# Second attention of a two-branch encoder layer: exponentials copied by ScalarE's DMA queue into a tile of the rounded type, transposed from there later in the tile; 15-row ranges

## The chip, the cores and the metric

The kernel runs on one core of one Trainium2 chip. The metric is the device time of one launch in microseconds. A core has five engines with a queue of instructions each: TensorE (PE, with its weight loads shown apart as PEld), VectorE (DVE), ScalarE (ACT), GpSimd (POOL) and SyncE (SP), which here only issues DMAs. Other engines can issue DMAs as well; before the change ACT does so twice, at the start.

## The reference

One layer over two sequences of 2048 tokens (x_prompt, x_sample) with 1024 features. All is float32.

```
h    = rms_norm(x) * norm_w
q_a | k_a | v_a | g_a | q_b | k_b | v_b | g_b = h @ w_in          # 3328 columns
A: windowed attention, 8 query heads on 2 key heads, +-128 tokens, norms, rotary, a sink per head
B: 8 heads on a grid of 32 rows x 64 columns; a query sees 8 rows x 16 columns around it
   q_b, k_b = rms_norm(q_b), rms_norm(k_b)
   s  = q_b . k_b / 8 + rpb_b[row offset, column offset];  p = softmax(s);  o_b = p @ v_b
x = x + concat(o_a * silu(g_a), o_b * silu(g_b)) @ w_out
y = x + (p @ w_ple) * sigmoid(x @ w_ple_gate)
```

## The kernel before, in words

Products are made in split form: a float32 operand is kept as a part rounded to PE's faster type (F32R in the code, fp32r in the profile's casts) and a rest, and three products of these parts are added (`project`, line 257). Casts and subtractions that make the two parts run on ACT, DVE and POOL.

The work has three stages. Tiles f = 0 to 31 are the first attention (about 0 to 800 us), tiles f = 32 to 95 the second (about 800 to 1815 us), and then follows the output stage. While a tile of attention runs, PE also makes projections for later tiles (the products `pq`, `pg`, and in the second attention `pqk`, `pvg`, at the end `pple`); they are a stream from which `paired` (line 1054) lets so many columns run and then puts in the next piece of the attention, after a plan. PLAN_B is that plan: a share of the tile, whether the piece belongs to the tile itself (1) or to the one before it (0), its kind and its index. All PE instructions stand in the order that the program writes them (`pinned`, line 237). The other engines' orders are made by a scheduler, but for the instructions marked `P(...)`, which stay where the program puts them.

A tile of the second attention (`unit_b`, line 845) has 128 queries (8 rows by 16 columns of the grid), four heads, and a window of keys of `nr` rows by 24 or 32 columns. Its pieces for each head: `sc` makes the scores in PSUM (`scb`, two products) and adds the bias and takes the maximum on DVE (`softmax`, line 264, into a tile `s` of which there are five); `exp` makes the four exponentials in place on ACT (`exps`, line 275, in the head order 0, 2, 1, 3) and then loads the values (`vw`); `pt` transposes the exponentials by 3 or 4 chunks of keys into one PSUM bank (`ptb`, with the identity in another row order, `rowwise`, as the moving operand), from which ACT makes the rounded part and DVE the rest (`p_t`, lines 899 and 900); `po` multiplies with the values (`pob`); `fin` applies the gate. `po` of the last two heads runs in the tile after. `prep` readies the queries and keys of a later tile (`pqtb`, `pktb`; L837, L755 and L756), and `proj_b` takes in the projections (`vb`, `qg`; L811, L820).

Where the window has 32 columns and the block of rows is not at the edge, `nr` is 16 and the scores are 512 columns wide; with 24 columns it is 15 and they are 360 wide.

`ptb`, `scb` and `pgtb` share three PSUM banks, `pob`, `pqtb` and `pktb` two, the projections three. SP issues all loads and stores of the stages: weight blocks (`ws`), tokens (`stx`), biases, values (`vw`, `v_d`). A DMA of SP or ACT takes the next of eight landing counters (DMAHW0 to DMAHW7 in the rows below), and is issued when the DMA that had that counter before has landed. At the start the identity `ident` and `rowwise` are made in F32 by POOL, and the input stages are loaded in an order that the scheduler makes.

Of the kernel before, what the change touches and what calls it, by code (L numbers as in the profile page):

```python
# [25 lines left out]
ROW_WIN = {0: (0, 12, 12), 1: (4, 16, 15), 2: (12, 16, 15), 3: (20, 12, 12)}  # L26
# [3 lines left out]
def window(b, cb):  # L30
    c0, nc_ = COL_WIN[cb]
    r0, wide, narrow = ROW_WIN[b]
    nr = wide if nc_ == 32 else narrow
    rows = 5 if nr == 15 else 4
    return r0, nr, c0, nc_, rows

# [9 lines left out]
def query_rows(b, cb, j):  # L46

    r0, _, _, _, rows = window(b, cb)
    k0 = r0 + rows * j
    see = [r for r in range(8) if k0 - 7 <= min(max(8 * b + r - 4, 0), 24) <= k0 + rows - 1]  # L50
    return (see[0], max(see[-1] + 1, 4)) if see[0] == 0 else (min(see[0], 4), see[-1] + 1)


def bias_offsets():
# [28 lines left out]
TW = 512  # L83
# [13 lines left out]
    (0.45, 1, "pt", 0), (0.52, 1, "pt", 1), (0.60, 1, "pt", 2), (0.66, 1, "po", 0), (0.74, 1, "pt", 3), (0.80, 1, "po", 1),  # L97
# [3 lines left out]
def emit(ctx, tc, io):  # L101
# [9 lines left out]
    ident = cp.tile([128, 128], F32, tag="ident", name="ident")  # L111
    make_identity(nc, ident)

    rowwise = cp.tile([128, 128], F32, tag="rowwise", name="rowwise")
    nc.gpsimd.tensor_copy(rowwise.rearrange("p (r c) -> p r c", c=16), ident.rearrange("p (c r) -> p r c", r=8))
# [138 lines left out]
    def tr(out, in_, eye=ident):  # L254
        pinned(nc.tensor.transpose(out, in_, eye))  # L255
# [19 lines left out]
    def exps(sm, fct, gs, sink=None):  # L275

        mx, nm, den, rd, ss = (sm[k] for k in ("mx", "nm", "den", "rd", "s"))
        if sink is None:
            nc.vector.tensor_scalar_mul(nm, mx, -1.0)  # L279
            yield  # L280
        else:
            nc.vector.scalar_tensor_tensor(out=nm, in0=mx, scalar=-1.0, in1=sink[1], op0=ALU.mult, op1=ALU.min)
        for n_, i in enumerate((0, 2, 1, 3) if sink is None else range(4)):
            ex = nc.scalar.activation(ss[i], ss[i], AF.Exp, bias=nm[:, i:i + 1], accum_out=den[:, i:i + 1])  # L284
            if sink is None and n_ == 0:
                P(ex)
        if sink is not None:
# [374 lines left out]
    p_rot = []  # L662

    def unit_a(f, kv):
# [6 lines left out]
        def sc(i):  # L671
# [3 lines left out]
            if half == 0:  # L675
                pairs.append(ap.tile([128, 640], F32, tag="ev", name="s2", bufs=3))
                if not right:
                    nc.gpsimd.memset(pairs[pair][:, 256:320], 0.0)
# [166 lines left out]
    def unit_b(f):  # L845
# [5 lines left out]
        kc, nch = rows * ncol, nr // rows  # L851
# [10 lines left out]
        def load_values():  # L862
# [4 lines left out]
            for j in range(nch):  # L867
                v = four[:, j] if spare else \
                    ap.tile([128, 4, 2 * HD], F32R, tag=("vp", "vr_")[j % 2], name="vw", bufs=3 - j % 2)
                nc.sync.dma_start(v[:kc].bitcast(F32).rearrange("p h d -> p (h d)"),  # L870
                                  v_d[half, s, cb][r0 + rows * j:r0 + rows * j + rows]
                                  .rearrange("r c h a d -> (r c) (h a d)"))
                vw.append(v)
# [6 lines left out]
        def sc(h):  # L880
# [5 lines left out]
            if h == 3:  # L886
                got["ex"] = exps(sm, hr_b[:, st:st + 1], gs)
                next(got["ex"])

        def pt(x):  # L890
            h = (0, 2, 1, 3)[x]
            pt = ptile([128, 512], "pt", "ptb")
            for j in order:

                c = at[j] - 16 * sees[j][0]
                tr(pt[:kc, c:c + 128], sm["s"][h][:, kc * j:kc * j + kc], rowwise)
# [6 lines left out]
        def po(x):  # L903
# [7 lines left out]
            for j in order[::-1]:  # L911
                a, z = sees[j]
                mm(po[:, i, :].rearrange("p (a q) -> p a q", a=2)[:, :, 16 * a:16 * z], vw[j][:kc, h, :],
                   p_ts[x][:kc, :, at[j]:at[j + 1]], j == order[-1], j == order[0])
# [66 lines left out]
    made = []  # L981
# [7 lines left out]
    def ple_ahead(n, tail=False):  # L989

        load_p(n + 1)
        for m in range(KT):
# [13 lines left out]
            else:  # L1006
                ev = ap.tile([128, TW], F32, tag=("ev", "sq")[m // 2 % 2], name="ev", bufs=3 - m // 2 % 2)
# [419 lines left out]
```

## Time and profile before

| | us |
|---|---|
| runs (three) | 2465.72, 2466.20, 2466.57; median 2466.2 |
| profiled execution, its span | 2462.8 |
| PE busy | 2451.7 (100%) |
| weight loads (PEld) busy | 2075.4 (84%) |
| DVE busy | 1704.7 (69%) |
| ACT busy | 1413.1 (57%) |
| POOL busy | 856.8 (35%) |

The span runs from the first to the last instruction that the profile shows; the run's time is taken from outside and is 3.4 us more at the median. Busy times count an engine's instructions from start to end. Matmuls overlap each other in the pipeline, so that PE's 100% says that it always has a product in flight, and not how fast the products follow each other: this is told by the distance of their starts. "L255 PE ptb" is the transposition at line 255, called for the tile `ptb`. In the lines of groups, `out<-in` names the tiles; `128x368 fp32r<-128x368 f32` are output and input, partitions by elements, with their types. In the chain of waits, each row has a start, a length and the work that held the end up in that time; `x4` says that four instructions of a kind stand in the row.

### The profile page before, as it was taken

The numbers are of one execution on the slowest core, as the hardware profiler recorded it, in microseconds if no ns is written. First come the engines' busy times: TensorE is split into PE (matmuls) and PEld (weight loads), VectorE is DVE, ScalarE is ACT, GpSimd is POOL, SyncE is SP. The second block draws the span as 40 slices with busy tenths as digits, with TensorE's granted clock in tenths as the row PEclk, the third lists the DMA queues.
The fourth block names the chain that finished last, engine by engine and source line by source line (L and its number), as shares of the span: only waits on it lengthen the run. The fifth ranks groups of instructions, "written<-read, shape, count | busy, mean of one in ns | idle before, by whom it ended". The sixth has DMA issues, their size and how long they took to land.

```text
span 2462.8 us, 40532 instructions
## 1 busy us (share of the span) xinstructions
PE 2451.7 (100%) x13062; PEld 2075.4 (84%) x13062; DVE 1704.7 (69%) x4214; ACT 1413.1 (57%) x3408; POOL 856.8 (35%) x1363
## 2 busy tenths in 40 slices
PE   9999999999999999999999999999999999999999
PEld 8888888888888888888888888888888888888887
DVE  7777777777765666666666666666537655677776
ACT  6777776777664665656655566665763222344433
POOL 4555555555543544454444444443100000000000
PEclk9999999999999999999999999999999999999999
DMA  6332223332255565556955566667977445856765
GB/s 228 123 103 93 95 89 103 95 101 88 95 180 166 167 192 182 183 163 195 314 187 183 170 219 202 193 199 242 317 248 262 154 165 178 270 180 206 251 222 171
DMA packets 243316, 442.01 MB, mean 179 GB/s; under 512 B 27904, under 2 KB 82592, under 8 KB 237856
## 3 DMA queue, kind: packets, MB, share of 16 engines
q1 hardware_dynamic: 242816, 439.42, 54.8%
q8 instruction: 104, 1.70, 0.3%
q14 instruction: 108, 0.88, 0.1%
q10 hardware_dynamic: 288, 0.01, 0.0%
HBM read 309.29 MB, written 134.23 MB: 180 GB/s over the span
## 4 chain that ended last, share of the span: by engine, by line
PE 94%; DVE 2%; ACT 2%; POOL 1%; issue 1%; DMA 1%; SPq 0%; ACTq 0%; POOLq 0%; DVEq 0%
PE pvg L252 15%; PE pqk L252 14%; PE acca L1230 14%; PE accc L1230 11%; PE pg L252 6%; PE pq L252 6%; PE scb L252 4%; PE ptb L255 4%; PE pple L252 4%; PE pob L252 3%; PE po L252 3%; PE pk L252 3%; PE sc L252 3%; PE pt L255 2%; DVE pr L712 1%
## 5 line engine op out<-in xcount | busy, mean ns | idle before, releaser
L284 ACT ACTIVATE s<-s,nm 128x320 f32<-128x320 f32 (+6 forms) x512 | 294.5, 576 | 318.5 <-DVE nm L279 198.9
L252 PE MATMUL pvg<-wb,xr 128*128 128x512 f32 x1536 | 461.5, 407 | 0.0
L252 PE MATMUL pqk<-wa,xr 128*128 128x512 f32 x1536 | 442.9, 411 | 0.0
L252 PEld LDWEIGHTS pqk<-wa,xr 128*128 128x128 f32 x1536 | 266.1, 189 | 36.7
L252 PEld LDWEIGHTS pvg<-wb,xr 128*128 128x128 f32 x1536 | 266.8, 189 | 30.8
L1212 ACT CAST opd<-raw 128x512 fp32r<-128x512 f32 x224 | 131.5, 618 | 271.7 <-PE acca L1230 118.0
L353 POOL TENSOR_TENSOR xr<-stx,xr 128x512 fp32r<-128x512 f32 x186 | 238.9, 1295 | 101.3 <-ACT xr L352 76.8
L1213 DVE TENSOR_TENSOR opd<-raw,opd 128x512 fp32r<-128x512 f32 x224 | 146.7, 687 | 146.9 <-ACT opd L1212 146.9
L252 PE MATMUL pg<-wb,xr 128*128 128x512 f32 x768 | 233.3, 410 | 1.0 <-DVE vv L510 1.0
L252 PE MATMUL pq<-wa,xr 128*128 128x512 f32 x768 | 219.3, 400 | 0.0
L268 DVE CUSTOM_DVE_ANT_0 s<-scb,bias 128x288 f32<-128x288 f32 (+3 forms) x256 | 142.2, 556 | 104.6 <-PE scb L252 101.7
L137 POOL TENSOR_TENSOR yb<-vrb,power 128x8 f32<-128x8 f32 x64 | 106.4, 1662 | 222.1 <-DVE vrb L784 202.4
L1230 PE MATMUL accc<-opd,wb 128*128 128x512 f32 x768 | 176.7, 389 | 0.0
L1230 PE MATMUL acca<-opd,wa 128*128 128x512 f32 (+1 forms) x780 | 175.9, 386 | 0.5 <-ACT r L1308 0.5
L1230 PE MATMUL acca<-opd,s 128*128 128x512 f32 x768 | 175.4, 389 | 0.0
L1230 PEld LDWEIGHTS acca<-opd,wa 128*128 128x128 f32 x780 | 145.0, 188 | 30.2 <-ACT r L1308 0.7
L1230 PEld LDWEIGHTS acca<-opd,s 128*128 128x128 f32 x768 | 144.2, 188 | 29.9
L1230 PEld LDWEIGHTS accc<-opd,wb 128*128 128x128 f32 x768 | 144.2, 188 | 29.9
L919 DVE TENSOR_TENSOR otb<-pob,otb 64x512 f32<-64x512 f32 x128 | 88.1, 688 | 113.2 <-ACT otb L918 111.5
L252 PEld LDWEIGHTS pob<-p_t,vw 128*128 128x128 f32 (+2 forms) x832 | 132.6, 189 | 23.4 <-DVE p_t L900 3.4
L252 PEld LDWEIGHTS pq<-wa,xr 128*128 128x128 f32 x768 | 135.2, 189 | 17.3
L712 DVE TENSOR_TENSOR pr<-pt,pr 128x512 fp32r<-128x512 f32 (+2 forms) x248 | 135.4, 549 | 15.9 <-ACT pr L710 12.5
(171 smaller groups left out, 5169.9 us busy)
## 6 DMA issues: line engine op xcount, KB each, us to landing
stx<-x_b SPq DMA_DIRECT2D x128, 256.0 KB
vw<-v_d SPq DMA_DIRECT2D x112, 256.0 KB
stx<-x_a SPq DMA_DIRECT2D x64, 256.0 KB
stn<-x_n SPq DMA_DIRECT2D x64, 256.0 KB
v_d<-vb SPq DMA_DIRECT2D x64, 256.0 KB
ple_d<-ev SPq DMA_DIRECT2D x64, 256.0 KB
xres<-x_r SPq DMA_DIRECT2D x64, 256.0 KB
x_d<-r SPq DMA_DIRECT2D x64, 256.0 KB
```

The costliest lines, as they stand in the source:

```text
L137: nc.gpsimd.tensor_tensor(out=y, in0=v, in1=power.broadcast_to([128, n]), op=ALU.pow)
L252: pinned(nc.tensor.matmul(out, lhsT, rhs, start=start, stop=stop))
L255: pinned(nc.tensor.transpose(out, in_, eye))
L268: nc.vector.tensor_tensor_reduce(out=s, in0=ps[:, :n], in1=bias, scale=1.0, scalar=-3.0e38, op0=ALU.add, op1=ALU.max, accum_out=sm["mx"][: ...
L284: ex = nc.scalar.activation(ss[i], ss[i], AF.Exp, bias=nm[:, i:i + 1], accum_out=den[:, i:i + 1])
L353: low.tensor_tensor(out=lo, in0=raw, in1=hi.bitcast(F32), op=ALU.subtract)
L712: nc.vector.tensor_tensor(out=pr[r, 1, to], in0=pt[r, c], in1=pr[r, 0, to].bitcast(F32), op=ALU.subtract)
L919: nc.vector.tensor_tensor(out=ot[a:a + 64], in0=pq[a:a + 64], in1=ot[a:a + 64], op=ALU.add)
L1212: P(nc.scalar.copy(hi, v))
L1213: P(nc.vector.tensor_tensor(out=lo, in0=v, in1=hi.bitcast(F32), op=ALU.subtract))
L1230: pinned(nc.tensor.matmul(ps[:, cols], w[k][:, a, c:c + 128], o[:, b, cols], start=i in (0, 1, 4) and k == 0 and j == 0, stop=k == 3 and j ...
```

## The change

1. The middle blocks of rows take 15 rows of keys with 32 columns too. Their scores are 480 columns wide in place of 512, cut into chunks of 4, 4, 3 and 4 rows (`chunks`), so that the number of transpositions stays. This meets 16 of the 64 tiles.
2. `ident` and `rowwise` are of the type F32R. They are cast from an F32 identity in a pool that is closed again. A transposition of an F32 tile reads them as F32; one of an F32R tile is done in that type (`tr`).
3. For f below 90 (58 of the 64 tiles, 756 of the 832 transpositions of `ptb`), each head's exponentials are copied from `s` to one tile `tn` of type F32R, by a DMA that ACT issues. All four exponentials and the four DMAs are held in program order: exponentials 1 and 2, the first DMA, exponential 3, the second DMA, exponential 4, the last two DMAs. These are 232 DMAs of 128 rows by 288 to 480 elements. The transpositions read `tn`.
4. In PLAN_B the pieces `pt` and `po` of a tile come later: `pt` at 0.68 to 0.90 of the tile in place of 0.45 to 0.74, `po` of the first two heads at 0.86 and 0.95 in place of 0.66 and 0.80. `po` of the last two heads keeps its place in the next tile (0.09, 0.16).
5. To make room, tiles of the tag `ev` (`s2` in the first attention, `tn`, `ev` at the end) share one space as one tile of three parts.

```diff
--- before.py
+++ after.py
@@ -23,16 +23,21 @@
 NEG = -1.0e30
 EPS = 1e-6
 
-ROW_WIN = {0: (0, 12, 12), 1: (4, 16, 15), 2: (12, 16, 15), 3: (20, 12, 12)}
+ROW_WIN = {0: (0, 12), 1: (4, 15), 2: (12, 15), 3: (20, 12)}
 COL_WIN = {0: (0, 24), 1: (8, 32), 2: (24, 32), 3: (40, 24)}
 
 
 def window(b, cb):
     c0, nc_ = COL_WIN[cb]
-    r0, wide, narrow = ROW_WIN[b]
-    nr = wide if nc_ == 32 else narrow
-    rows = 5 if nr == 15 else 4
+    r0, nr = ROW_WIN[b]
+    rows = 5 if nr == 15 and nc_ == 24 else 4
     return r0, nr, c0, nc_, rows
+
+
+def chunks(nr, rows):
+
+    first = list(range(0, nr - rows, rows)) + [nr - rows]
+    return [(k, min(rows, z - k)) for k, z in zip(first, first[1:] + [nr])]
 
 
 def row_type(b):
@@ -45,9 +50,9 @@
 
 def query_rows(b, cb, j):
 
-    r0, _, _, _, rows = window(b, cb)
-    k0 = r0 + rows * j
-    see = [r for r in range(8) if k0 - 7 <= min(max(8 * b + r - 4, 0), 24) <= k0 + rows - 1]
+    r0, nr, _, _, rows = window(b, cb)
+    k, n = chunks(nr, rows)[j]
+    see = [r for r in range(8) if r0 + k - 7 <= min(max(8 * b + r - 4, 0), 24) <= r0 + k + n - 1]
     return (see[0], max(see[-1] + 1, 4)) if see[0] == 0 else (min(see[0], 4), see[-1] + 1)
 
 
@@ -94,7 +99,7 @@
 PLAN_B = (
     (0.00, 1, "sc", 0), (0.03, 1, "sc", 1), (0.07, 1, "sc", 2), (0.09, 0, "po", 2), (0.11, 1, "sc", 3), (0.16, 0, "po", 3),
     (0.16, 1, "exp", 0), (0.24, 0, "fin", 0), (0.35, 1, "prep", 0),
-    (0.45, 1, "pt", 0), (0.52, 1, "pt", 1), (0.60, 1, "pt", 2), (0.66, 1, "po", 0), (0.74, 1, "pt", 3), (0.80, 1, "po", 1),
+    (0.68, 1, "pt", 0), (0.75, 1, "pt", 1), (0.82, 1, "pt", 2), (0.86, 1, "po", 0), (0.90, 1, "pt", 3), (0.95, 1, "po", 1),
 )
 
 
@@ -108,11 +113,12 @@
         tag = PSM.get(tag, tag)
         return pp.tile(shape, F32, tag=tag, name=name, bufs=PSB[tag])
 
-    ident = cp.tile([128, 128], F32, tag="ident", name="ident")
-    make_identity(nc, ident)
-
-    rowwise = cp.tile([128, 128], F32, tag="rowwise", name="rowwise")
-    nc.gpsimd.tensor_copy(rowwise.rearrange("p (r c) -> p r c", c=16), ident.rearrange("p (c r) -> p r c", r=8))
+    ident, rowwise = (cp.tile([128, 128], F32R, tag=n, name=n) for n in ("ident", "rowwise"))
+    with tc.tile_pool(name="eye", bufs=1) as ep:
+        eye_ = ep.tile([128, 128], F32, tag="eye", name="eye")
+        make_identity(nc, eye_)
+        nc.vector.tensor_copy(ident, eye_)
+        nc.gpsimd.tensor_copy(rowwise.rearrange("p (r c) -> p r c", c=16), eye_.rearrange("p (c r) -> p r c", r=8))
     nw = cp.tile([128, KT], F32, tag="nw", name="nw")
     nc.scalar.dma_start(nw, io["norm_w"])
     ms_a = cp.tile([128, 2 * NT], F32, tag="ms_a", name="ms_a")
@@ -252,7 +258,10 @@
         pinned(nc.tensor.matmul(out, lhsT, rhs, start=start, stop=stop))
 
     def tr(out, in_, eye=ident):
-        pinned(nc.tensor.transpose(out, in_, eye))
+        if in_.dtype == F32R:
+            pinned(nc.tensor.transpose(out.bitcast(F32R), in_, eye))
+        else:
+            pinned(nc.tensor.transpose(out, in_, eye.bitcast(F32)))
 
     def project(ps, xr, w, cost):
 
@@ -272,7 +281,7 @@
     def sm_tiles():
         return {"s": [], **{k: ap.tile([128, 4], F32, tag=k, name=k, bufs=3) for k in ("mx", "nm", "den", "rd")}}
 
-    def exps(sm, fct, gs, sink=None):
+    def exps(sm, fct, gs, sink=None, turned=None):
 
         mx, nm, den, rd, ss = (sm[k] for k in ("mx", "nm", "den", "rd", "s"))
         if sink is None:
@@ -280,10 +289,18 @@
             yield
         else:
             nc.vector.scalar_tensor_tensor(out=nm, in0=mx, scalar=-1.0, in1=sink[1], op0=ALU.mult, op1=ALU.min)
+        waiting = []
         for n_, i in enumerate((0, 2, 1, 3) if sink is None else range(4)):
             ex = nc.scalar.activation(ss[i], ss[i], AF.Exp, bias=nm[:, i:i + 1], accum_out=den[:, i:i + 1])
-            if sink is None and n_ == 0:
+            if sink is None and (n_ == 0 or turned is not None):
                 P(ex)
+            if sink is None and turned is not None:
+                waiting.append(i)
+                for k in waiting[:1] if n_ in (1, 2) else waiting[:] if n_ == 3 else ():
+                    to = turned[:, k, :ss[k].shape[-1]]
+                    P(nc.scalar.dma_start(to.bitcast(F32), ss[k]))
+                    ss[k] = to
+                    waiting.remove(k)
         if sink is not None:
             es = ap.tile([128, 4], F32, tag="es", name="es", bufs=3)
             nc.vector.tensor_tensor(out=es, in0=sink[0], in1=nm, op=ALU.add)
@@ -659,7 +676,7 @@
         qrest[f] = split_q(pqt, q1, q2, 1)
         return q1, q2
 
-    p_rot = []
+    p_rot, s2, tn = [], [], []
 
     def unit_a(f, kv):
         s, t = divmod(f, NT)
@@ -673,7 +690,10 @@
             a, z = span[half]
             c0, n = 128 * t - 128 + 64 * half, z - a
             if half == 0:
-                pairs.append(ap.tile([128, 640], F32, tag="ev", name="s2", bufs=3))
+                if not s2:
+                    s2.extend([ap.tile([128, 3, 640], F32, tag="ev", name="s2", bufs=1), 0])
+                pairs.append(s2[0][:, s2[1] % 3])
+                s2[1] += 1
                 if not right:
                     nc.gpsimd.memset(pairs[pair][:, 256:320], 0.0)
             ps = ptile([128, 512], "sc", "sc")
@@ -848,7 +868,8 @@
         b, cb = divmod(j, 4)
         _, gs = held[f]
         r0, nr, c0, ncol, rows = window(b, cb)
-        kc, nch = rows * ncol, nr // rows
+        kc, ch = rows * ncol, chunks(nr, rows)
+        nch, kn = len(ch), [ncol * n for _, n in ch]
         n = nr * ncol
         if cb != 2:
             off, _ = BIAS_OFF[(row_type(b), col_type(cb))]
@@ -867,8 +888,8 @@
             for j in range(nch):
                 v = four[:, j] if spare else \
                     ap.tile([128, 4, 2 * HD], F32R, tag=("vp", "vr_")[j % 2], name="vw", bufs=3 - j % 2)
-                nc.sync.dma_start(v[:kc].bitcast(F32).rearrange("p h d -> p (h d)"),
-                                  v_d[half, s, cb][r0 + rows * j:r0 + rows * j + rows]
+                nc.sync.dma_start(v[:kn[j]].bitcast(F32).rearrange("p h d -> p (h d)"),
+                                  v_d[half, s, cb][r0 + ch[j][0]:r0 + sum(ch[j])]
                                   .rearrange("r c h a d -> (r c) (h a d)"))
                 vw.append(v)
 
@@ -884,7 +905,9 @@
                    ks_b[h % 2][:, r0:r0 + nr, h // 2, c0:c0 + ncol], j == 0, j == 1)
             softmax(h, ps, n, bias[:, h, :n], sm)
             if h == 3:
-                got["ex"] = exps(sm, hr_b[:, st:st + 1], gs)
+                if not tn:
+                    tn.append(ap.tile([128, 4, 480], F32R, tag="ev", name="tn", bufs=1))
+                got["ex"] = exps(sm, hr_b[:, st:st + 1], gs, turned=tn[0] if f < 6 * NT - AHEAD - 1 else None)
                 next(got["ex"])
 
         def pt(x):
@@ -893,7 +916,8 @@
             for j in order:
 
                 c = at[j] - 16 * sees[j][0]
-                tr(pt[:kc, c:c + 128], sm["s"][h][:, kc * j:kc * j + kc], rowwise)
+                k0 = ncol * ch[j][0]
+                tr(pt[:kc, c:c + 128], sm["s"][h][:, k0:k0 + kc], rowwise)
             p_t = main.tile([128, 2, 512], F32R, tag="p_t", name="p_t", bufs=3)
             hi, lo, pf = p_t[:kc, 0, :at[-1]], p_t[:kc, 1, :at[-1]], pt[:kc, :at[-1]]
             nc.scalar.copy(hi, pf)
@@ -910,8 +934,8 @@
             po, ot = got["po"], got["ot"]
             for j in order[::-1]:
                 a, z = sees[j]
-                mm(po[:, i, :].rearrange("p (a q) -> p a q", a=2)[:, :, 16 * a:16 * z], vw[j][:kc, h, :],
-                   p_ts[x][:kc, :, at[j]:at[j + 1]], j == order[-1], j == order[0])
+                mm(po[:, i, :].rearrange("p (a q) -> p a q", a=2)[:, :, 16 * a:16 * z], vw[j][:kn[j], h, :],
+                   p_ts[x][:kn[j], :, at[j]:at[j + 1]], j == order[-1], j == order[0])
             if i == 1:
                 a, z = 64 * e, 64 - 64 * e
                 pq = po.rearrange("p i (a q) -> p i a q", a=2)
...
             else:
-                ev = ap.tile([128, TW], F32, tag=("ev", "sq")[m // 2 % 2], name="ev", bufs=3 - m // 2 % 2)
+                if not evs:
+                    evs.extend([ap.tile([128, 3, 640], F32, tag="ev", name="ev", bufs=1), 0])
+                if m // 2 % 2:
+                    ev = ap.tile([128, TW], F32, tag="sq", name="ev", bufs=2)
+                else:
+                    ev = evs[0][:, evs[1] % 3, :TW]
+                    evs[1] += 1
             P(nc.scalar.copy(ev, ps))
```

On ACT, in the 39th tile of the second attention (the exponentials `s` with the sums `den` are those of L284 before and L294 now, `otb` is the output of the tile before, `q1b` belongs to `prep`), there stood before:

```order
L284 ACTIVATE s,den<-s,nm 128x512
L918 COPY otb<-pob 64x512
L284 ACTIVATE s,den<-s,nm 128x512 x3
L837 ACTIVATE q1b<-pqtb,wk 64x256
L216 CAST pre<-pre 128x512
L837 ACTIVATE q1b<-pqtb,wk 64x256
L899 CAST p_t<-ptb 128x368
L811 ACTIVATE vb<-pvg,rs_b 128x4x64
L755 CAST ks_b_9851<-pktb 64x2x16x8
```

The same place now, with what each instruction waits for (the counters are DMAHW0 to 7, the engines' own semaphores the others):

```order
L942 COPY otb<-pob 64x512 [waits PE_49]
L294 ACTIVATE s,den<-s,nm 128x480 [waits DVE_49]
L294 ACTIVATE s,den<-s,nm 128x480 [waits DMAHW4_49]
L301 DMA tn<-s 128x480 [waits DMAHW7_49,DMAHW2_49,Activation_49]
L294 ACTIVATE s,den<-s,nm 128x480
L301 DMA tn<-s 128x480 [waits DMAHW1_49,Activation_49]
L294 ACTIVATE s,den<-s,nm 128x480 [waits DMAHW5_49]
L301 DMA tn<-s 128x480 [waits DMAHW3_49,Activation_49]
L301 DMA tn<-s 128x480 [waits DMAHW6_49,DMAHW4_49,Activation_49]
```

Four DMAs with waits on landing counters now stand among the exponentials on ACT.

On PE, in the same tile, the first transpositions up to the first `pob` stood before with these products of the projection between them:

```order
L255 MATMUL ptb<-rowwise,s 128x128 x4
L252 MATMUL pvg<-wb_15821,xr 128x512 x2
L255 MATMUL pktb<-ident,kb 128x128 x2
L252 MATMUL pqk<-wa_15589,xr 128x512
L255 MATMUL ptb<-rowwise,s 128x128 x4
L252 MATMUL pqk<-wa_15589,xr 128x512 x2
L252 MATMUL pqk<-wa_15591,xr 128x512 x2
L255 MATMUL ptb<-rowwise,s 128x128 x4
L252 MATMUL pqk<-wa_15591,xr 128x512
L252 MATMUL pqk<-wa_15593,xr 128x512 x2
L252 MATMUL pob<-p_t,vw 128x256
```

and now with these:

```order
L262 MATMUL ptb<-rowwise,tn 128x128 x4
L258 MATMUL pqk<-wa_15568,xr 128x512 x3
L262 MATMUL ptb<-rowwise,tn 128x128 x4
L258 MATMUL pqk<-wa_15570,xr 128x512 x3
L258 MATMUL pqk<-wa_15572,xr 128x512
L262 MATMUL ptb<-rowwise,tn 128x128 x4
L258 MATMUL pqk<-wa_15572,xr 128x512 x2
L258 MATMUL pob<-p_t,vw 128x256
```

Between the first `ptb` and the first `pob` there are now nine products of the projection in place of ten and two transpositions of `pktb`; these stand ahead of the first `ptb` now.

On SP the program started with these loads (`stx` the tokens, `ws` and `wg` weight blocks, `stn` the tokens for the norm's sums):

```order
L335 DMA stx<-x_a 128x512
L232 DMA ws<-w_in 128x2x256
L335 DMA stx<-x_a 128x512
L232 DMA ws<-w_in 128x2x256 x3
L335 DMA stx<-x_a 128x512 x2
L232 DMA ws<-w_in 128x2x512 x4
L335 DMA stn<-x_n 128x512 x2
L232 DMA wg<-w_in 128x512 x4
```

and now starts with these:

```order
L238 DMA ws<-w_in 128x2x512 x2
L238 DMA wg<-w_in 128x512 x4
L424 DMA rw<-rope_w 128x64
L446 DMA snk_all<-sink 128x8
L352 DMA stx<-x_a 128x512
L238 DMA ws<-w_in 128x2x256
L352 DMA stx<-x_a 128x512
L238 DMA ws<-w_in 128x2x256 x3
L352 DMA stx<-x_a 128x512 x2
L238 DMA ws<-w_in 128x2x512 x2
```

Six weight loads (two of 512 KB, four of 256 KB) and two small ones now stand ahead of the first tokens.

2 lines of the change are left out of this document (1 added, 1 removed).

## The prediction

> **What bounds the kernel now.** I read the page first, for its engines and its chain of waits.
>
> ```profile
> span 2462.8 us, 40532 instructions
> PE 2451.7 (100%) x13062; PEld 2075.4 (84%) x13062; DVE 1704.7 (69%) x4214; ACT 1413.1 (57%) x3408; POOL 856.8 (35%) x1363
> PE 94%; DVE 2%; ACT 2%; POOL 1%; issue 1%; DMA 1%; SPq 0%; ACTq 0%; POOLq 0%; DVEq 0%
> ```
>
> 94% of the chain is PE's own work. Then the table by stretches, and the chain of waits cut to the second attention with its projections (800 to 1740 us; columns after the stretch: PE, PEld, DVE, ACT, POOL busy, PE's clock, DMA share, GB/s).
>
> ```profile
> 800.00:1740.00 940.00, 940.00 (x5119) 790.41 (x5118) 628.92 (x1592) 577.13 (x1356) 430.45 (x493) 1.00 0.64 202
> by line: PE pvg L252 34.8%; PE pqk L252 34.3%; PE scb L252 9.0%; PE ptb L255 8.8%; PE pob L252 8.1%; PE pktb L255 1.3%; PE pgtb L255 1.3%; PE pqtb L255 1.3%; PE pple L252 0.9%
> ```
>
> In these 940 us the chain holds nothing but PE. So a nanosecond that a PE instruction gets shorter there is a nanosecond of the end, work put on ACT or the DMA engines is free until PE waits for it, and there is no wait to be taken away: the later places of the pieces can cost but not bring. The chain's own rows in one tile (start, length, work) give PE's prices:
>
> ```profile
> 1400.67 0.44 PE ptb L255 x4
> ...
> 1403.84 0.69 PE pqk L252 x3
> 1404.54 0.40 PE pob L252 x4
> 1404.94 0.98 PE pqk L252 x4
> 1405.92 0.44 PE ptb L255 x4
> ...
> 1407.45 2.14 PE pqk L252 x9
> 1409.59 0.48 PE scb L252 x2
> ```
>
> A 512-column product costs 0.235 us (2.14/9), a transposition 0.110 (0.44/4; the share of ptb, 8.8% of 940 us, over 756 says 0.109), a pair of 512-column scores 0.48.
>
> **The transpositions in the rounded type.** This is the term that decides. 756 transpositions of `ptb` change type. The trace has no transposition of that type, but it has products of it with 128 to 256 columns: `pob`. Behind a group of them the next products are late: four pqk take 0.98 where 4 x 0.235 is 0.94, so 0.04 us belongs to pob, and its four cost 0.44. A group of three, in another tile, and the columns of the groups (groups by line in 1340.4 to 1341.0 us, then in 1421.6 to 1422.3 us, a group of four like the one at 1404.54):
>
> ```profile
> 1340.56 0.30 PE pob L252 x3
> 1340.85 0.98 PE pqk L252 x4
> ```
> ```profile
> L252 PE MATMUL pob<-p_t,vw 128*128 128x256 f32 x2 | 0.4, 280 | 0.0
> L252 PE MATMUL pob<-p_t,vw 128*128 128x128 f32 x1 | 0.2, 223 | 0.0
> ```
> ```profile
> L252 PE MATMUL pob<-p_t,vw 128*128 128x128 f32 x2 | 0.3, 254 | 0.0
> L252 PE MATMUL pob<-p_t,vw 128*128 128x256 f32 x1 | 0.3, 280 | 0.0
> L252 PE MATMUL pob<-p_t,vw 128*128 128x224 f32 x1 | 0.3, 262 | 0.0
> ```
>
> Three with 640 columns cost 0.34, four with 736 cost 0.44: 0.113 and 0.110 each. By columns alone (0.235/512 = 0.46 ns each) it would be 0.294 and 0.338. So a product of the rounded type does not come under about 0.11 us, however few its columns. The rows of weight loads name a candidate:
>
> ```profile
> L252 PEld LDWEIGHTS pob<-p_t,vw 128*128 128x128 f32 x448 | 70.1, 189 | 11.4 <-DVE p_t L900 0.8 <-ACT xr L352 0.5
> L255 PEld LDWEIGHTS ptb<-rowwise,s 128*128 128x128 f32 x448 | 56.7, 140 | 15.6
> L255 PEld LDWEIGHTS ptb<-rowwise,s 128*96 128x96 f32 x192 | 23.1, 126 | 8.6 <-ACT s L284 0.2
> ```
>
> A load in the rounded type (pob) takes 189 ns, one in F32 (ptb) 140. The rounded type moves its columns faster and loads its weights slower, and a transposition is one load for 128 columns. Bounds: columns alone, 128 x 0.46 = 59 ns, saves 51 x 756 = 39 us; a load 49 ns longer that shows in full costs 49 x 756 = 37 us. Between them I take the nearest row, the small products of the same type, 0.113 where it was 0.109: **+3 us**.
>
> The Trainium skill (page "TensorE: Matmul & The Clock Gate", section "LDWEIGHTS (loading the stationary operand)") gives a load's time by its columns, P / 1.2 ns, so 107 ns for 128 and 80 for 96. For pob the trace agrees with it as a pace (110 to 113 ns). By it alone a rounded transposition of 96 columns would cost 80 ns and one of 120 columns 100, an estimate of some 7 us saved in place of 3 lost.
>
> **Scores of 480 columns.** 64 pairs (16 tiles by 4 heads) shrink by 32/512 of 0.48 = 0.03 us: **-2 us**. The softmaxes and exponentials get shorter beside PE.
>
> **The start.** The first products of the projection wait for tokens and weights:
>
> ```profile
> 5.36 7.99 PE L252 MATMUL pk<-wx,xr 128*128 128x256 f32 x48
> 13.18 11.07 PE L252 MATMUL pq<-wa,xr 128*128 128x512 f32 x48
> ```
> ```profile
> 3.74 0.62 ACT L352 CAST xr<-stx 128x512 fp32r<-128x512 f32 x1 [0.81 <-DMA stx<-x_a]
> 11.08 2.68 ACT L151 ACTIVATE wa<-ws,nw 128x512 fp32r<-128x512 f32 x4 [0.78 <-DMA ws<-w_in]
> ```
>
> The first tokens are there at 3.74 us. From then to 11.08 landed seven blocks of 256 KB and the first of 512 KB, 2.3 MB in 7.3 us. The change puts 2 x 512 + 4 x 256 KB = 2 MB ahead of the tokens, so they come 2/0.31 = 6.5 us later. Nothing covers this: PE has no other work there. Some comes back, since the weights are then there (pk's 48 took 7.99 us; at half of 0.235 they need 5.6): 4 us if all does. Two casts of wa that now stand ahead on ACT (0.67 each, 2.68/4) make it 8. I take **+6**.
>
> **Copies, their waits and the later places.** ACT issues 232 DMAs. What an issue holds its queue is seen at the start, and what the exponentials and the casts behind them take, in the timeline around 1414 us:
>
> ```profile
> 1.15 0.47 ACTq L125 DMA_DIRECT2D wkt<-qk_norms  x1
> ```
> ```profile
> 1417.20 0.71 ACT L284 ACTIVATE s<-s,nm 128x512 f32<-128x512 f32 x1
> 1419.40 0.47 ACT L899 CAST p_t<-ptb 128x368 fp32r<-128x368 f32 x1
> 1420.26 0.60 ACT L755 CAST ks_b<-pktb 64x256 fp32r<-64x256 f32 x1
> ```
> ```profile
> 1420.92 0.54 DVE L900 TENSOR_TENSOR p_t<-ptb,p_t 128x368 fp32r<-128x368 f32 x1
> 1421.49 0.64 DVE L756 TENSOR_TENSOR ks_b<-pktb,ks_b 64x256 fp32r<-64x256 f32 x1
> ```
>
> 4 x 0.47 = 1.9 us a tile, 108 us in 58 tiles, on an ACT busy 577 of 940: it fits. How long a copy takes from issue to landing no row says; the ends are a tiny load and a block of 512 KB under load:
>
> ```profile
> 0.72 3.18 DMA nw<-norm_w
> 4.77 6.28 DMA ws<-w_in
> ```
>
> A tile is 17.3 us long here (pqk x9 at 1407.45, the next at 1424.76):
>
> ```profile
> 1424.76 2.13 PE pqk L252 x9
> ```
>
> The first copy is issued behind the second exponential, about 1416.5; the first `ptb`, before at 1417.98, comes 0.23 x 17 = 4 us later, near 1422. That leaves 5.4 us: enough for a landing of 3.2, not for one of 6.3. An issue of ACT also waits till the DMA eight places back in SP and ACT together has landed, which binds where SP loads weights in bursts. ACT's exponentials, p_t and projections' casts (vb, ks_b) are queued behind it, and PE waits for these. I put 1 us on each of two such tiles: **+2** (0 to 10).
>
> Between first `ptb` and first `pob` PE has three groups (1.32) and nine products (2.12): 3.44 us. In that time must run: the group (0.44), ACT p_t (0.47), ACT ks_b (0.60), DVE ks_b (0.64), which now stands ahead, and DVE p_t (0.54): 2.69. Slack is 0.75 us, less what semaphores take; were it all used and one more cast and subtraction ahead (0.60 + 0.64), each of 58 tiles would wait 0.5 us, 29 us. I take 0.07 a tile: **+4** (0 to 29).
>
> **Sum.** 2462.8 + 3 - 2 + 6 + 2 + 4 = 2475.8 us of span. The three runs had a median 3.4 us above the span (2466.2): **2479 us**, slower by 0.5%. Its own range, with the start at 4 to 8, the places at 0 to 12 and the pace 105 to 116 ns, is 2468 to 2492.
>
> **Rivals.** *A: the rounded type is cheaper in a transposition.* The 0.11 of pob would be its own weight load; a transposition could load as the F32 one does (140 ns, not 189) and move columns at 0.46 ns, and then 128 columns cost 59 to 80 ns. I put 69: -40 x 756 = -30 us. For it: an F32 transposition of 96 columns loads faster (126 against 140) and yet its pace is the same 0.11 (the groups of three took 0.33), so not the load sets its pace but something else, perhaps the moving columns, and these the rounded type speeds up. Against it: no product of that type under 0.11. Time: 2479 - 3 - 30 = 2446. The skill's page named above ("Weight-path perf modes — Fast Weight Load (FWL) and DoubleRow") says that loads are sped up when the type is not FP32 and the columns are 128, which speaks for A; the rows disagree, 189 against 140.
>
> *B: the last quarter is too narrow.* The pieces pt to po1 now lie in 0.68 to 0.95 and the next tile's scores at 0.00 need the three banks back. If the evacuations (0.47 + 0.54 for each of four heads, beside the softmaxes of the next tile) fall behind, each tile waits the 0.5 us above: 2479 + 25 = 2504. For it: DVE at 629 of 940 is the busiest after PE. Against: the slack of 0.75.
>
> *C: half of A.* The pace falls to about 90 ns, by the load's columns or the like: -19 x 756 = -14 us, and what is lost at the start eats it: 2479 - 3 - 14 = 2462.
>
> **Chances.** Forecast 0.42, A 0.34, B 0.10, C 0.14. About 0.2% (5 us) can be told from no change: faster is below 2461, slower above 2471. Faster: nearly all of A and half of C, 0.38; same: the rest of C and a little of the forecast, 0.12; slower: 0.50. The range leaves out the lower part of A and most of B: 2443 to 2492; the forecast's own is 2468 to 2492.
>
> **What would show it.** In the chain of waits of the second attention: ptb x4 stays at 0.44 to 0.46 (A: 0.24 to 0.32) and its share of the 940 us near 9% (A: 5 to 6%). pk starts at 10 to 13 us in place of 5.36. PE's waits on the DMA to `tn` and on p_t stay under 10 us together (B: 25 and more). The first attention, whose instructions keep their order, should keep its length. I am wrong if ptb gets shorter by a third, or if the first tokens come no later.

## The result, and the profile after

The changed kernel takes 2546.0 us (median of four runs, 2537.4 to 2549.8) against 2466.0 before: 1.032 times as long, with a 95% interval of 1.030 to 1.034. Slower was forecast, at 2479; the loss is 80 us and not 13. First the page of the changed kernel:

```profile
span 2545.8 us, 40929 instructions
PE 2469.8 (97%) x13062; PEld 2073.9 (81%) x13062; DVE 1704.6 (67%) x4215; ACT 1413.7 (56%) x3408; POOL 851.1 (33%) x1363
```

PE now stands idle for 76 us of its span, where it was 11, and its busy time has grown by 18 us though nothing was added. The waits, PE's and then those of its weight loads (what waited, on what: us in total, times, longest), and the transpositions by form:

```profile
PE ptb L262 <- DMA tn<-s: 44.9, 46, 2.8
PE pk L258 <- issue: 6.8, 1, 6.8
PE pob L258 <- DVE p_t L924: 3.5, 7, 0.9
```
```profile
PEld ptb L262 <- DMA tn<-s: 63.9, 52, 3.2
```
```profile
L262 PE MATMUL ptb<-rowwise,tn 128*128 128x128 f32 x408 | 51.7, 246 | 22.5 <-DMA tn<-s 22.4
L262 PE MATMUL ptb<-rowwise,tn 128*96 128x128 f32 x168 | 19.5, 225 | 3.1 <-DMA tn<-s 3.1
L264 PE MATMUL ptb<-rowwise,s 128*128 128x128 f32 x40 | 6.3, 272 | 0.0
```

PE waits for the copies in `tn`: 46 times, up to 2.8 us. A transposition in the rounded type is shorter than one in F32 (246 ns on the mean, with those at a lowered clock in it, against 272). One tile shows the course of it. First come the issues of copies in ScalarE's queue (`...` stands for rows left out), then PE, then the table by stretches (PE, PEld, DVE, ACT, POOL busy, PE's clock, DMA share, GB/s):

```profile
1461.52 0.52 ACTq L301 DMA_DIRECT2D tn<-s  x1
1462.20 0.50 ACTq L301 DMA_DIRECT2D tn<-s  x1
...
1463.61 0.69 ACTq L301 DMA_DIRECT2D tn<-s  x1
```
```profile
1468.34 0.54 PE L262 MATMUL ptb<-rowwise,tn 128*128 128x128 f32 x4 [1.77 <-DMA tn<-s]
1468.71 0.93 PE L258 MATMUL pqk<-wa,xr 128*128 128x512 f32 x3
1469.48 0.53 PE L262 MATMUL ptb<-rowwise,tn 128*128 128x128 f32 x4
1469.85 2.02 PE L258 MATMUL pqk<-wa,xr 128*128 128x512 f32 x4
```
```profile
1460.00:1464.00 4.00, 4.00 (x21) 3.25 (x21) 1.82 (x5) 3.44 (x9) 0.87 (x2) 1.00 0.68 186
1464.00:1468.00 4.00, 2.56 (x13) 1.73 (x11) 2.97 (x6) 2.44 (x5) 1.57 (x4) 1.00 0.99 306
1468.00:1472.00 4.00, 3.66 (x18) 2.86 (x19) 1.93 (x4) 2.43 (x5) 0.83 (x1) 0.73 1.03 392
1472.00:1476.00 4.00, 4.00 (x24) 3.50 (x24) 1.09 (x3) 1.90 (x4) 1.73 (x2) 0.84 0.40 128
```

The first copy is issued at 1461.52 and lands at 1468.29 by its landing counter; the transposition that needs it starts at 1468.34, 6.8 us after the issue. The 16 DMA engines are busy nearly all the time from 1464 to 1472 (share 0.99 and 1.03). And the wait has a second price: after 1.77 us without work the granted clock is 0.73 and 0.84 on the mean in the next two stretches of 4 us, and a row of four products of 512 columns takes 2.02 us, where the one at 1450.90 took 1.16. In the clock record of the trace this is one stretch of 3.41 us at 0.50, from 1469.9 on; there are twelve such stretches, one of them twice as long, between 900 and 1850 us. That is where the added busy time comes from, as the products `pqk` show, the same 1536 before and now:

```profile
L252 PE MATMUL pqk<-wa,xr 128*128 128x512 f32 x1536 | 442.9, 411 | 0.0
```
```profile
L258 PE MATMUL pqk<-wa,xr 128*128 128x512 f32 x1536 | 464.2, 420 | 0.0
```

Tile by tile, from the starts of the first scores in both traces, most tiles in which PE doesn't wait for `tn` get up to 0.5 us shorter than before, and the 34 in which it waits get 0.2 to 5.2 us longer. The 58th and the 61st get 4.8 and 3.8 us longer without such a wait. Together it is 72 us over the 63 tile lengths between the first scores of the first tile and those of the last. The offset at the first of them is 9.3 us, nearly all of it from the start:

```profile
12.05 0.55 PE L258 MATMUL pk<-wx,xr 128*128 128x256 f32 x1 [6.80 <-issue]
13.08 8.64 PE L258 MATMUL pk<-wx,xr 128*128 128x256 f32 x47 [0.48 <-DVE wx L158]
21.56 11.07 PE L258 MATMUL pq<-wa,xr 128*128 128x512 f32 x48
```
```profile
14.00:20.00 6.00, 6.00 (x33) 5.96 (x33) 5.13 (x12) 4.40 (x11) 0.00 (x0) 0.57 1.01 325
```

pk starts 6.7 us later, as the order of the loads says, but it gets no time back from weights that are there: behind the 6.8 us of idleness its clock is 0.57. pq starts 8.4 us later than before.

### The profile page after: what moved, and what is told of

It is laid out like the page before. It is cut to its first block, busy times and chain, and to the rows that moved or that the text cites. A ratio compares the mean times of both kernels' runs of the same rounds, so it can differ in the third digit from the quotient of the medians.

```text
span 2545.8 us, 40929 instructions
## 1 busy us (share of the span) xinstructions
PE 2469.8 (97%) x13062; PEld 2073.9 (81%) x13062; DVE 1704.6 (67%) x4215; ACT 1413.7 (56%) x3408; POOL 851.1 (33%) x1363
## 5 line engine op out<-in xcount | busy, mean ns | idle before, releaser
L258 PE MATMUL pqk<-wa,xr 128*128 128x512 f32 x1536 | 464.2, 420 | 0.0
L258 PE MATMUL pvg<-wb,xr 128*128 128x512 f32 x1536 | 449.0, 405 | 0.0
L294 ACT ACTIVATE s<-s,nm 128x320 f32<-128x320 f32 (+6 forms) x512 | 293.4, 574 | 131.7 <-DVE nm L291 118.8
L924 DVE TENSOR_TENSOR p_t<-ptb,p_t 128x368 fp32r<-128x368 f32 (+5 forms) x256 | 122.8, 488 | 135.7 <-ACT p_t L923 133.9
L942 ACT COPY otb<-pob 64x512 f32<-64x512 f32 x128 | 74.3, 581 | 209.2 <-PE pob L258 208.9
L923 ACT CAST p_t<-ptb 128x368 fp32r<-128x368 f32 (+5 forms) x256 | 107.6, 426 | 138.4 <-PE ptb L262 127.4
L262 PEld LDWEIGHTS ptb<-rowwise,tn 128*128 128x128 f32 (+2 forms) x756 | 86.6, 140 | 98.6 <-DMA tn<-s 63.9
```

What stands on the lines that cost most here:

```text
L258: pinned(nc.tensor.matmul(out, lhsT, rhs, start=start, stop=stop))
L262: pinned(nc.tensor.transpose(out.bitcast(F32R), in_, eye))
L923: nc.scalar.copy(hi, pf)
L924: nc.vector.tensor_tensor(out=lo, in0=pf, in1=hi.bitcast(F32), op=ALU.subtract)
L942: nc.scalar.copy(ot[a:a + 64], pq[z:z + 64])
```

## The experiments

Landing times below are from the trace's records of the landing counters: from the start of a DMA's issue to the counter's last step before its next issue. They were read in the second attention alone.

**Four kernels that take the change apart.** `start_ok` changes where the F32 identity lies (and makes it behind the pool main):

```
-    with tc.tile_pool(name="eye", bufs=1) as ep:
-        eye_ = ep.tile([128, 128], F32, tag="eye", name="eye")
...
+    eye_ = main.tile([128, 2, 512], F32R, tag="p_t", name="p_t", bufs=3)[:, 0, :128].bitcast(F32)
```

> The changed kernel with one edit: the F32 identity from which ident and rowwise are cast lies in a slot of the tag p_t (first used in the second attention) and not in a pool that is closed again, so that the first tokens are loaded ahead of the weights as before. The first projection pk starts near 5.4 us in place of 12.05, and the offset of the first attention against the kernel before (8 to 9 us) goes. If the start is a term of its own: 2537 us. If PE makes the lost time good elsewhere, or the start hangs on something else: 2546.

Measured: 2525.3 (2522.0 to 2535.0), 1.024 [1.022, 1.026]. The offset at the first tile of the second attention is 1.5 us in place of 9.3, so the start is worth 8 us. The medians differ by 21, more than was expected. The two profiled executions (2545.8 and 2533.2) differ by 13, of which 8 lie at the start and 5 in the second attention; the runs of the two kernels spread by 12 and 13 us, so that what lies beyond the start is not told from that spread.

`no_copy` passes `turned=None` to `exps` for all tiles.

> The changed kernel without the copies: the transpositions read s in F32, as before, at the new late places of PLAN_B, with the 15-row ranges and the new start. Theory 1 (PE waits for copies that land late, and runs at a lower granted clock behind each wait): the waits go, 2466 + 8 (start) - 2 (scores) + 0 to 4 = 2472 to 2476. Theory 2 (the late places leave no room for the evacuations or the banks): stays above 2500.

Measured: 2483.9 (1.0065 [1.005, 1.008]). The offset against before is 8.4 us at the first tile of the second attention and 11.0 at its 60th: the later places cost some 3 to 5 us, counting the scores' gain; another 5 come in the last five tiles, 3.5 of them in the 61st, where PE waits 2.7 us for DVE's softmax. So the time lies 8 us above what the first theory gave, and far below the second: the later places as the main cause are ruled out.

`copy_unread` leaves out one line, so that the transpositions read `s`:

```
                     P(nc.scalar.dma_start(to.bitcast(F32), ss[k]))
-                    ss[k] = to
```

> The changed kernel with all 232 copies issued and landing, but the transpositions read s in F32, so nothing on PE waits for a copy. Theory 1 (waiting for the landing): close to the kernel without copies, at most 5 us more, 2472 to 2481. Theory 3 (the copies' issues hold ACT, and their traffic holds the loads, whoever reads them): most of the 80 us stays, 2520 to 2550.

Measured: 2491.0 (1.0093 [1.008, 1.011]). So 55 of the 80 us go when nothing waits for the copies, though they are still made. This kernel also transposes in F32; copy_f32 below, which does so too but waits, puts the price of the wait at 49. The 7 us above no_copy are 2 more than the first theory allowed. The tiles show two places of loss, 8 us in the 26th and 27th tile and 8 in the 58th, where weights are loaded; in the other tiles this kernel is the shorter one. ScalarE's rows in the first of these:

```profile
1216.57 0.70 ACT L294 ACTIVATE s<-s,nm 128x480 f32<-128x480 f32 x1 [2.38 <-DMA v_d<-vb]
...
1237.63 3.78 ACTq L301 DMA_DIRECT2D tn<-s  x2
1241.45 0.47 ACT L856 ACTIVATE q1b<-pqtb,wk 64x256 fp32r<-64x256 f32 x1 [5.44 <-DMA tn<-s]
```

ScalarE's queue stands for 2.4 us at a store of SP, and for 5.4 us around two copies. By the landing records each of these issues follows the landing of the DMA that had its counter before: at 1215.97 a store of `v_d`, at 1237.55 a load of `vw`, and at 1240.86 ScalarE's own copy of 1233.88. The casts behind them wait too.

`copy_f32` makes `tn` a tile of F32.

> The changed kernel with tn of the type F32: the same copies, waited for as in the changed kernel, but transposed in F32. It prices the rounded transposition. Three groups of the rounded type in the changed kernel cost 0.25 to 0.28 us where F32 costs 0.327. If all of this counts, 756 transpositions by 0.019 us = 14 us: 2560. If the waits for the landing absorb it (PE would only have waited longer): 2546 to 2552.

Measured: 2539.8 (1.029 [1.028, 1.031]), a miss on both counts: not longer than the changed kernel but 6 us shorter by the medians, which the runs' spread of 12 and 7 us hardly tells from equal. PE's wait for `tn` sums to the same:

```profile
PE ptb L264 <- DMA tn<-s: 44.9, 44, 2.6
```

Different is the mean granted clock, 0.998 here and 0.989 there: 5 and 28 us, if the missing share is taken of the whole span. The stretches at 0.50 are three here and twelve there between 900 and 1850 us, though the waits are alike. That the lower clock took what the rounded transposition saves would fit these numbers, but is not shown, and why the clock holds better with the same waits in F32 stays open.

no_copy, copy_unread, copy_f32 and the changed kernel form a ladder. no_copy is 16 us above the runs of before that were made with it; the copies, made but not read, add 7; to read and wait for them adds 49 (2539.8 against 2491.0); the rounded type adds 6, within the spread.

**Where the copies' time goes.** In start_ok the copies land 5.7 us after their issue (median; one copy in ten over 7.4), and the tiles fall into some near 3.8 and some near 7.

`late` moves the transpositions on: `pt` at 0.84, 0.89, 0.94 and 0.99, `po` of all heads in the next tile at 0.02, 0.07, 0.12 and 0.16, on start_ok.

> The kernel start_ok with the transpositions later still: pt at 0.84 to 0.99 of the tile, po of all four heads in the next tile (0.02 to 0.16). That gives each copy about 2.6 us more (0.16 of 16.5 us) before it is waited for; copies of the changed kernel landed 3.5 to 8.3 us after their issue, with a median of 5.8, and the first transposition was due about 5 us after. Theory 1 (only the landing is late): the waits for tn fall from 100 us to under 20 and the time to 2470 to 2485. Theory 2 (the last quarter is too narrow): more waits on p_t and banks in place of these, 2500 and more.

Measured: 2483.2 (1.007 [1.006, 1.009]). With 2.6 us more for each copy the loss against before falls from 57 to 17 us. The waits of the tile tn's readers (PE and its weight loads) for the copies were 109.5 us in start_ok, and now:

```profile
  DMA tn<-s: 24.2, 34
  DVE p_t L923: 19.2, 29
```

The first row is a little above the 20 us that were expected. The second row is the narrow quarter of the second theory: it appears, and is small. 11 us lie in the tiles with weight loads (3 in the 26th and 27th, 8 in the 58th and 59th).

`values_later` issues the loads of `vw` at 0.48 of the tile (a piece of its own in PLAN_B), `late_values` joins this to `late`.

> The kernel start_ok with one edit: the loads of the values (four of up to 256 KB a tile) are issued at 0.48 of the tile and not right with the copies. Theory 1a (copies are slow because they share the 16 DMA engines with the values' burst; these were busy 0.99 to 1.03 in 1464 to 1472 us): the copies land about 4 us after their issue, and the time falls by most of the wait, to 2475 to 2495. Theory 1b (a copy from SBUF to SBUF in rows under 2 KB is slow by itself, or waits at its issue for a landing counter): 2515 to 2530.

> Both edits on start_ok: the pieces of late, and the values at 0.48. If the landing is the only cause, no wait for tn is left and the rounded transpositions show: 2467 - 14 - 2 = 2451, plus up to 15 where SP's weight loads hold ACT's queue (tiles 24 to 27 and 56 to 59): 2451 to 2470. If something else of the change costs too, above 2475.

Measured: 2527.2 and 2486.3, where start_ok has 2525.3 and late 2483.2: nothing gained, a miss for both. The copies still land after 5.4 and 5.3 us. It is not the values' burst.

`no_bias` loads the biases for the first two tiles only, `quiet` adds the later values:

```
-            nc.sync.dma_start(bt[-1][:, :, :n], io["bias"][half][:, off:off + 4 * n].rearrange("p (h n) -> p h n", h=4))
+            if len(bt) < 4:
+                nc.sync.dma_start(bt[-1][:, :, :480], io["bias"][half][:, :1920].rearrange("p (h n) -> p h n", h=4))
```

> The kernel start_ok with the biases of the second attention loaded for its first two tiles only; left out are the other loads of 576 to 960 KB (the scores then take a bias of another tile). In start_ok the biases' landing has a median of 7.9 us and the copies' 5.7, with tiles near 3.7 and tiles near 7.4. Theory 1a' (the copies share the DMA engines with the biases' load that is issued at the same time): the copies land in about 4 us in all tiles and the time falls from 2525 to 2475 to 2490. Theory 1b (the copies are slow by themselves, or at the counters): 2515 to 2530.

> The same with the values loaded at 0.48 of the tile too, so that in the first third of a tile the copies have hardly a load beside them. If contention is all: copies at 3.5 to 4 us, no wait for tn outside the tiles with weight loads, 2455 to 2475. If it equals the kernel without biases, the values' loads do nothing.

Measured: 2467.7 (1.0009 [1.000, 1.002]) and 2470.9. The copies land after 3.9 and 3.7 us. PE's wait for `tn` is 11.7 us in quiet; in start_ok and no_bias it is

```profile
PE ptb L261 <- DMA tn<-s: 44.2, 50, 2.4
```
```profile
PE ptb L261 <- DMA tn<-s: 6.7, 10, 1.5
```

So the loads of 576 to 960 KB, which SP issues near the copies (in start_ok copy at 1451.94, bias at 1452.08, copy at 1452.62), seem to be what the copies wait behind. start_ok itself says the same, if its tiles are parted by the place of the load (the 24th to 28th and those from the 56th on, where weights are loaded, left out). In 13 tiles no bias is loaded near the copies, and these land after 3.8 us in the median. In 13 the load is issued 1.5 us ahead of the first copy: 4.6 us. In 24 it is issued from 0.9 us ahead of the first copy to 0.6 us behind it: 6.9 us, and 48 of the 67 us that the tiles get longer lie in these 24. But no_bias and quiet also move fewer bytes.

`bias_moved` keeps the bytes and moves the load behind the stores of `v_d`, at about 0.8 of the tile before the one that needs it; `bias_early` puts it in that place one tile earlier still. Both keep the load in program order (`load_bias` is the old load as a function; bias_early calls it with f + 2):

```
-    (0.16, 1, "exp", 0), (0.24, 0, "fin", 0), (0.35, 1, "prep", 0),
+    (0.16, 1, "exp", 0), (0.24, 0, "fin", 0), (0.35, 1, "prep", 0), (0.50, 1, "bias", 0),
...
-                "exp": lambda _: (next(got["ex"]), load_values())}
+                "exp": lambda _: (next(got["ex"]), load_values()), "bias": lambda _: load_bias(f + 1, P)}
```

> The kernel start_ok with the same loads of the biases, but issued behind the stores of the values at about 0.8 of the tile before, in place of right between the copies. If the coincidence makes the copies late: they land in about 4 us, and the time falls from 2525 to near the kernel without these loads, 2466 to 2478. If the bytes do it wherever they are: above 2500. A bias that comes too late for the next tile's softmax would show as a wait of DVE on the bias.

> As bias_moved, with each bias loaded a whole tile earlier (for the tile after next), so that it is there in time; same bytes, not beside the copies. If the coincidence of copies and bias load was the cause: no wait of DVE on the bias, copies in about 4 us, 2466 to 2478, as without the bias loads. If bytes count wherever they are: above 2490.

Measured: bias_moved 2539.2, worse than start_ok, and bias_early 2470.5 (1.0019 [1.001, 1.003]). In both the copies land after 3.8 and 3.9 us. In bias_moved PE's wait for `tn` shrinks to 8.6 us, but a new one takes its place, on DVE's softmax and, behind it, on PE's scores:

```profile
DVE s L276 <- DMA bias<-bias: 60.7, 32, 4.8
```
```profile
PE scb L257 <- DVE mx L276: 45.4, 29, 4.2
PE ptb L261 <- DMA tn<-s: 8.6, 12, 1.4
```

In bias_early that wait is gone:

```profile
PE ptb L261 <- DMA tn<-s: 11.5, 15, 1.8
PE pple L257 <- DVE qg L840: 2.2, 1, 2.2
```

Same bytes, same copies, another place for 46 loads: 2525 becomes 2470. The coincidence was the cause.

`bias_early_skip` makes no copies in the 24th to 28th and 56th to 58th tile; `late_skip` is the same exception on `late`.

> As bias_early, and no copies in the 24th to 28th and 56th to 58th tile, which load weights. If late landing and these tiles are the whole loss: the kernel before less 2 us for scores and some 11 us for the rounded transpositions of 50 tiles, 2453 to 2460. If not, above 2464.

> The kernel late with no copies, and F32 transpositions, in the tiles that load weights beside them (24th to 28th and 56th to 58th). In late these tiles lose 5 to 6 and 8 to 9 us. If that loss is ACT's queue held by the copies' waits for counters: 2483 - 14 + 1 = 2470, near the kernel before. If it comes from the later places: 2480 to 2484.

Measured: 2462.8 (0.9989 [0.998, 0.9998]) and 2473.4 (1.003 [1.002, 1.005]), 8 and 10 us less than without the exception. Both lie 3 us above what was expected. In bias_early_skip the second attention is 8.5 us ahead of before at its 60th tile; 5 us of that are lost in the last four tiles and the change to the output stage, and why is not settled.

`bias_skip` is the same exception on bias_moved, and has the wait of that kernel:

> The kernel bias_moved without copies, with F32 transpositions, in the tiles that load weights beside them (24th to 28th and 56th to 58th). The late landing and these tiles together are the whole loss, if what is left is the kernel before less 2 us for scores and less some 11 us for the rounded transpositions of 50 tiles: 2453 to 2460. If not, above 2464.

Measured: 2529.6; DVE waits 58.9 us for the bias.

**The prices alone.** `rows15` is start_ok without copies and with PLAN_B's old places; `act_round` lets ScalarE write the exponentials into `tn`, rounded, without any DMA, at the old places:

```
-            ex = nc.scalar.activation(ss[i], ss[i], AF.Exp, bias=nm[:, i:i + 1], accum_out=den[:, i:i + 1])
+            to = ss[i] if turned is None else turned[:, i, :ss[i].shape[-1]]
+            ex = nc.scalar.activation(to, ss[i], AF.Exp, bias=nm[:, i:i + 1], accum_out=den[:, i:i + 1])
...
+            ss[i] = to
```

> The 15-row ranges alone: the kernel start_ok with no copies, F32 transpositions of s and PLAN_B's old places. Forecast of this term was 64 x 0.03 = 2 us off: 2464. If the exponentials or the softmaxes count: lower; if nothing: 2466.

> The kernel start_ok without any DMA for the exponentials: ScalarE writes them, rounded, into tn, and PLAN_B has its old places. What is left out is the part of the exponentials below the rounding; the sums still take in what ScalarE adds up. It prices the rounded transposition with no wait: 756 x 0.019 = 14 us and the scores 2 us off the kernel before, 2451 (2446 to 2456). If the rounded type only seemed cheaper in stretches at a lower clock or behind waits: 2464 to 2468.

Measured: rows15 2469.5 (1.0013 [1.000, 1.002]), a miss: the shorter scores gain 0.8 us in the first 24 tiles, and lose it again where weights are loaded. act_round 2451.1 (0.9940 [0.9925, 0.9955]), as expected, and 15 us faster than before, by 0.6%. The chain of waits of act_round, in one tile:

```profile
1397.22 0.29 PE ptb L261 x4
1397.51 0.77 PE pqk L257 x3
1398.28 0.41 PE pob L257 x4
1398.69 2.13 PE pqk L257 x9
1400.82 0.45 PE scb L257 x2
```

Four transpositions take 0.29 us, and the three products behind them 0.77 where 3 x 0.235 is 0.705: 0.36, or 0.09 each, where F32 takes 0.11. Over the tiles, act_round gains 16 us on rows15 between the first tile and the 60th: 21 ns for each of 756.

## Why the prediction was wrong, by its own steps

**What bounds it** held: PE's own pace, with no wait to take away. What the rounded type can bring where nothing waits is the transpositions' 16 us (act_round against rows15).

**The transpositions: +3 forecast, -16 measured.** The sign was wrong. I took the price of the rounded type from `pob`, its nearest row, and named its weight load (189 ns) as the candidate for the reason. The loads of the rounded transpositions are not like pob's:

```profile
L261 PEld LDWEIGHTS ptb<-rowwise,tn 128*128 128x128 f32 x408 | 47.7, 141 | 13.6
L261 PEld LDWEIGHTS ptb<-rowwise,tn 128*96 128x96 f32 x168 | 17.9, 125 | 7.6
```

141 and 125 ns in act_round, as in F32 (140 and 126). So the longer load of pob does not come with the type alone, as rival A had it. The gain is C's size and not A's: 88 ns on the mean and not 69. Groups of three with 96, 120 and 128 columns of weights cost 0.247, 0.268 and 0.280 us in act_round (with the delay of the next product counted in), 0.327 in F32 whatever the columns: the pace falls with the columns of the load. The Trainium skill's rule (page "TensorE: Matmul & The Clock Gate", section "LDWEIGHTS (loading the stationary operand)"), by which the load goes by columns, has this direction, but its 107 and 80 ns for 128 and 96 columns stand against 93 and 82 here; the prediction's estimate of 7 us saved by that rule had the sign right and half of the size.

**Scores: -2 forecast.** 0.45 for the pair against 0.48, as worked out; the whole kernel shows nothing of it (rows15).

**The start: +6 forecast, 8 measured.** The late tokens were right. What I counted as coming back (pk with its weights there) went to the clock: 0.57 behind the idle stretch. The Trainium skill's page named above (section "HAM oscillation — how this bites in real kernels") says that a PE left idle long enough is throttled when it starts again, and the trace agrees. No step of the prediction had a price for it, though a wait for PE was in the sum.

**Copies and ACT's queue: +2 forecast, 62 measured** (2546.0 against 2483.9 of no_copy, with the transpositions' gain in it). This is the step that failed. The prediction had the frame: 5.4 us from the first issue to the transposition, and landings from 3.2 to 6.3 us. It then chose as if the short end held, and gave 1 us to each of two tiles; none of its rivals had late copies either. The copies landed 5.8 us after issue in the median, 50 of the 232 after more than 7, and the wait for them cost 49 us in F32 (copy_f32 against copy_unread) and 55 in the changed kernel. What was not looked at is what SP issues in the same microseconds: the bias of 576 to 960 KB. It stands in the order of SP's instructions beside the values, and its load in the kernel before lands 6.2 us after its issue in the median. The tiles with weight loads cost 16 us (copy_unread; to leave the copies out there brought 8 to 10), not 2; there the reason was the one named, ACT's issues held by landings, most of them SP's.

**The later places: +4 forecast,** 3 to 5 measured (no_copy). Rival B, the narrow quarter, was small even with the still later places (19 us of the transpositions' waits on p_t in `late`, of which 17 fell on PE's weight loads and 3 on its products).

Of the signs that the prediction named, the tokens' came true (pk at 12.05 us). The waits on `tn` and p_t were to stay under 10 us together and are 48, and ptb x4 was to stay at 0.44 to 0.46 and takes 0.36 where nothing waits (act_round): neither the forecast's value nor A's 0.24 to 0.32, but C's 90 ns each.

So the forecast came out on the right side by luck: it put the loss on a transposition that gains and on the start, and most of the loss was the landing.

## What to carry to other kernels

A copy on the DMA engines that PE waits for must be priced with what else is issued in the same few microseconds, not with a quiet row: here one load of up to 960 KB beside it turned 3.8 us into 6.9 (start_ok's medians), and a tile's slack of 5 us into a loss. When such a load is moved away, ask at once who waits for it: bias_moved exchanged one wait for another of the same size, and only bias_early, a tile ahead, paid. And if an engine writes the operand anyway, have it write the type that the next engine wants; with the exponentials rounded by ScalarE, which leaves out their part below the rounding, that took 15 us off and needed no DMA.

## What the runs showed of the hardware

A wait of PE can cost more than its length: after 1.77 us of idleness the granted clock was 0.50 for 3.41 us, and after 6.8 us at the start 0.57 on the mean of 14 to 20 us. It doesn't always: in copy_f32 no such stretch follows PE's wait of 1.99 us that ends at 1229.76, and what decides it is not shown. Over the changed kernel the mean clock was 0.989, which is 28 us of the span; its runs with 0.995 took 2537 us, those near 0.990 2544 to 2550. The runs of the changed kernel spread by 12 us, those of act_round by 3.

A transposition in the rounded type costs 0.082 to 0.093 us by the columns of its operand, in F32 0.109 with 96, 120 or 128 (act_round and before). In the kernel before, groups of three and four products of the rounded type, with 128 to 256 columns each, came to 0.113 and 0.110 a product.

An engine that issues DMAs gives its own queue to the landings of others: ScalarE stood 5.4 us with casts behind it because the counters that it shares with SP were held by DMAs that had not landed.
